# Full-width products of ones on TensorE ahead of norm 1, and one copy that moves on GpSimd

## The chip, the cores and the metric

The kernel runs on one core of one Trainium2 chip. Its time is the device time of one execution in microseconds, and a verdict compares medians of runs. TensorE (PE in the profile) multiplies matrices and writes to PSUM banks; VectorE (DVE), ScalarE (ACT) and GpSimd (POOL) do the elementwise work; SyncE (SP) issues most of the transfers. Each engine works through its own list of instructions in order and waits on semaphores for the others.

## The reference, cut to what matters

One transformer block on 512 tokens of width 1024: an RMS norm, one wide projection that feeds a state-space mixer and a sparse-attention mixer, a gated merge, a convolutional feed-forward part, and a gated embedding. The change touches only the stretch around the first norm and the first projection:

```
def rmsnorm(x, g):
    xf = x.astype(jnp.float32)
    y = xf * lax.rsqrt(jnp.mean(xf * xf, axis=-1, keepdims=True) + EPS)
    return (y * g.astype(jnp.float32)).astype(x.dtype)
...
    n1 = rmsnorm(h, g_mix[i])
    z = n1 @ w_in[i]
```

and, because an instruction of it is moved, the state-space mixer's small tables: `dt = exp(log_dt)`, `a_bar = exp(lam * dt)` and what follows from them.

## The kernel before, in words

The 512 tokens are four tiles of 128 rows (`xts[0..3]`). The gain vector of norm 1 (`grow`, one row of 1024) is spread over 128 partitions by two products of a row of ones with it, into two PSUM banks (`gbs`, L331). Per token tile, the sum of squares goes through `rstd_of` on VectorE (L343, L352, L355), `x_scaled` multiplies the tile by that and by the gains in two halves on VectorE (L300), `t_high` transposes it on TensorE into PSUM (L308) and ScalarE copies it to `n1h`, rounded (L311, by `copy`, L76), and `t_low` takes the remainder `n1l` on VectorE (L316, by `tt`, L55). Three passes of products per tile follow (`v_passes`, L282): `n1h` with the rounded weights, `n1l` with the rounded weights, and, after all tiles, `n1h` with the weights' remainder (`WV` part 1, made by `wv_lo`, L274).

The order on TensorE, VectorE and ScalarE is written by hand in the block from L328 on: an engine's instructions stand there in the order of the code. So on ScalarE the copies of `pps` (the transposed small parameter rows: `prm`, `dcol`) stand ahead of the squares of tile 1, and these ahead of the copies to `n1h` of tile 0. On GpSimd and SyncE, and after this block, a scheduler puts the instructions in order from its own estimates of when each can start.

GpSimd computes the state-space mixer's small vectors (128x16) from `prm`: a chain of two dependent instructions per step of a polynomial (`stg`, `exp_of`, `ts`, `tt`) that starts at `lre` and ends at `rho`, with `kk` and `fl` on the way. VectorE takes them up after the third pass's weights: `ang` from `kk`, `at` from `fl`, then the square of `rho`, and then some thirty small instructions of sine and cosine. Into GpSimd's chain the scheduler puts one instruction that belongs elsewhere: `W2d`, a copy of a 128x64 weight that SyncE loads (`W2`, L711, L714).

`pps` is one of the two PSUM banks with the tag "t" (L336), `ident` a unit matrix, and `sq` a scratch tile for squares.

Of the kernel before, what the change touches and what calls it, by code (L numbers as in the profile page):

```python
# [10 lines left out]
F32R = mybir.dt.float32r  # L11
# [7 lines left out]
P = 128  # L19
# [26 lines left out]
def hybrid_kernel(ctx: ExitStack, tc: tile.TileContext, A, out):  # L46
    nc = tc.nc
    V, G, S, PE = nc.vector, nc.gpsimd, nc.scalar, nc.tensor
# [26 lines left out]
    def copy(o, a):  # L75
        S.activation(o, a, AF.Copy)  # L76
# [10 lines left out]
    def pool(name, bufs=1, side=None, space=None):  # L87
        kw = {"name": name, "bufs": bufs, "reuse_waits": "tile"}
        if side:
            kw["side"] = side  # L90
        if space is not None:
            kw["space"] = space
        return tc.tile_pool(**kw)
# [7 lines left out]
    def bank(tag, name):  # L101
        return psp.tile([P, 512], F32, tag=tag, name=name, bufs=BANKS[tag])
# [17 lines left out]
    def rstd_of(ss, ss2=None, n=1):  # L120

        v, y, t = (small(f"r{c}{n}", n) for c in "vyt")
        ts(v, ss, 0.0 if ss2 is None else ss2, D * EPS, ADD, ADD)
        ts(y.bitcast(I32), v.bitcast(I32), -0.5, FIRST, MUL, ADD)
        for a in NEWTON[:3]:
            if n == 1:
                stt(t, y, v, y, MUL, MUL)
            else:
                tt(t, y, y, MUL)
                tt(t, t, v, MUL)  # L130
            stt(y, t, 3 * a * a, y, SUB, MUL)
        return y
# [6 lines left out]
    def halves(t):  # L139
        return [t[:, i * 512:i * 512 + 512] for i in range(2)]  # L140
# [29 lines left out]
    def last(engine):  # L170
        return next(i for i in reversed(nc.cur_bb.bb.instructions) if i.engine == engine)
# [60 lines left out]
    px = sX.enter_context(pool("x", 1, "right"))  # L232
    xall = slot(cp, "h16", [P, NQ, D], F32, "xall")
    xts = [xall[:, qt] for qt in range(NQ)]
    sq = px.tile([P, D], F32, name="sq")
    wv0 = slot(py, "y8", [P, 2, KD, P], F32, "wv0")
    grow = wv0[0:1, 1].rearrange("p a b -> p (a b)")
    ones = pP.tile([1, P], F32, name="ones")
    G.memset(ones, 1.0)
    grow2 = pP.tile([2 * KD, P], F32, name="grow2")  # L240
    gains = cp.tile([P, 2, KD], F32, name="gains")

# [26 lines left out]
    def wv(x, i):  # L269
        _, w0, w, raw = VCOLS[i]  # L270
        return WV[:, x, :, w0:w0 + w], raw

    def wv_lo(i):
        tt(wv(1, i)[0], wv(1, i)[1], wv(0, i)[0], SUB)  # L274

    def v_passes(qt, passes):
        if qt not in vps:
            vps[qt] = bank(either(), "vps")
        for n in passes:
            nn, x = ((n1h, 0), (n1l, 0), (n1h, 1))[n]  # L280
            for k in range(KD):
                PE.matmul(vps[qt][:, :280], nn[:, k, qt * P:(qt + 1) * P], WV[:, x, k], start=n + k == 0,  # L282
                          stop=n == 2 and k == KD - 1)

    def v_out(qt):
        ps = vps[qt]
        vv = VV[:, qt].rearrange("p b g x d -> p (b g) x d")
        split(vv[:, :, 0], vv[:, :, 1], ps[:, 0:256].rearrange("p (a d) -> p a d", d=HD))
        S.activation(gates[:, qt], ps[:, 256:280], AF.Tanh, scale=0.5)
        ts(gates[:, qt], gates[:, qt], 0.5, 0.5, MUL, ADD)  # L290

    def squared(qt):
        S.activation(sq, xts[qt], AF.Square, accum_out=ss4[:, qt:qt + 1])
# [4 lines left out]
    def x_scaled(qt, r):  # L298
        for i, x in enumerate(halves(xts[qt])):
            stt(x, x, r, gbs[i], MUL, MUL)  # L300

    def t_high(qt):

        res = []
        for b in range(2):
            ps = bank("t", "nt")
            for k in range(4):
                PE.transpose(ps[:, k * P:(k + 1) * P], xts[qt][:, (4 * b + k) * P:(4 * b + k + 1) * P], ident)  # L308
            o = (slice(None), slice(4 * b, 4 * b + 4), slice(qt * P, qt * P + P))
            res.append((o, ps.rearrange("p (k t) -> p k t", k=4)))  # L310
            copy(n1h[o], res[-1][1])  # L311
        return res

    def t_low(res):
        for o, ps in res:
            tt(n1l[o], ps, n1h[o], SUB)  # L316
# [3 lines left out]
    def u_split(ct, part):  # L320
        if not part:
            uw.append([pw.tile([P, KD * P], F32R, name=n, tag=n).rearrange("p (k c) -> p k c", k=KD)
                       for n in ("wh", "wl")])
            copy(uw[ct][0], uraw[ct])
        else:
            tt(uw[ct][1], uraw[ct], uw[ct][0], SUB)

    with tc.manual_schedule(engines={mybir.EngineType.PE, mybir.EngineType.Activation, mybir.EngineType.DVE}):  # L328
        gbs = [bank("s", f"gb{i}") for i in range(2)]
        for ps, g in zip(gbs, halves(grow)):  # L330
            PE.matmul(ps, ones, g, start=True, stop=True)  # L331
        x0 = halves(xts[0])
        S.activation(sq[:, :512], x0[0], AF.Square, accum_out=ss4[:, 0:1])
        V.tensor_tensor_reduce(out=sq[:, 512:], in0=x0[1], in1=x0[1], scale=1.0, scalar=0.0, op0=MUL, op1=ADD,
                               accum_out=ss4[:, NQ:])
        pps = bank("t", "pps")  # L336
        for i in (2, 0, 1):
            PE.transpose(pps[:, i * 16:(i + 1) * 16], prow[:, i], ident[:NPAIR, :NPAIR])
        PE.transpose(pps[:, 48:52], drow, ident[:4, :4])
        copy(*wv(0, 0))  # L340
        copy(prm.rearrange("p a b -> p (a b)"), pps[:, :48])
        copy(dcol, pps[:, 48:52])
        x_scaled(0, rstd_of(ss4[:, 0:1], ss4[:, NQ:]))  # L343
        squared(1)
        t0 = t_high(0)
        V.tensor_copy(*wv(0, 1))
        v_passes(0, (0,))
        t_low(t0)
        v_passes(0, (1,))
        squared(2)  # L350
        squared(3)
        x_scaled(1, rstd_of(ss4[:, 1:2]))  # L352
        t1_ = t_high(1)
        v_passes(1, (0,))
        r = rstd_of(ss4[:, 2:4], n=2)  # L355
        t_low(t1_)
        v_passes(1, (1,))
        x_scaled(2, r[:, 0:1])
        t2_ = t_high(2)
        x_scaled(3, r[:, 1:2])  # L360
        v_passes(2, (0,))
        t3_ = t_high(3)
        t_low(t2_)
        v_passes(2, (1,))
        v_passes(3, (0,))
        t_low(t3_)
        v_passes(3, (1,))
        for i in range(2):
            u_split(i, 0)
        for i in range(2):  # L370
            wv_lo(i)
        u_split(0, 1)
        for qt in range(NQ):
            v_passes(qt, (2,))
            v_out(qt)
            if qt == 1:
                u_split(1, 1)
                trig_at = last(mybir.EngineType.DVE)
# [174 lines left out]
    for lv in range(5):  # L553
        n = 1 << lv
# [32 lines left out]
    for ct in range(4):  # L587
# [3 lines left out]
        for j in range(L):  # L591
            n = L - 1 - j
# [937 lines left out]
```

## Time and profile before

| | |
|---|---|
| median of 3 runs | 828.83 us (828.5 to 829.4) |
| the profiled execution | 829.46 us, of which the span from first to last instruction is 827.5 us |
| TensorE busy | 807.9 us, 98% of the span |
| VectorE, ScalarE, GpSimd busy | 524.3, 393.5, 255.2 us |
| transfers | 83.67 MB, mean 101 GB/s |

The times of rows are microseconds from the start of the span. A row of the timeline gives the start, the length, the engine, the line of the code, the instruction, what it writes and reads, how many it merges, and in brackets the idle time of the engine before it with what ended it. "f32" products with one row of weights take several passes each and appear as two records.

### The profile page before, as it was taken

How to read it: one execution, taken by the hardware profiler on the slowest of the kernel's cores; microseconds unless marked ns; L12 is line 12 of the kernel's file. 1: busy time of each engine (PE TensorE's matmuls, PEld its weight loads, DVE VectorE, ACT ScalarE, POOL GpSimd, SP SyncE). 2: the span in 40 equal slices, each digit the busy share in tenths (PEclk: the TensorE clock that was granted, in tenths of full speed). 3: DMA queues.
4: the chain of work that ended last, by engine and by line, in shares of the span. 5: the costliest groups of instructions: out<-in, count | busy, mean ns of one | idle time of the engine just before them, and what ended most of it. 6: DMA issues, size and time to landing. Idle time of an engine off the chain costs nothing. (4 is left out here: it accounts for less than half of the span.)

```text
span 827.5 us, 12241 instructions
## 1 busy us (share of the span) xinstructions
PE 807.9 (98%) x4529; PEld 677.7 (82%) x4529; DVE 524.3 (63%) x1088; ACT 393.5 (48%) x728; POOL 255.2 (31%) x314
## 2 busy tenths in 40 slices
PE   7999999999999999999999999999999999999996
PEld 5877888878888888888898888888888888888885
DVE  6899988377677640685454444444455947898744
ACT  4437553445777753434354444444434433565522
POOL 6595111124555533131032333333333100000411
PEclk9999999999999999999999999999999999999998
DMA  9663322522333423344052333233323342423011
GB/s 244 161 166 103 91 65 65 129 76 77 77 77 83 148 55 96 109 137 118 2 175 80 103 101 100 86 95 103 99 86 95 121 143 93 153 87 117 26 52 51
DMA packets 112001, 83.67 MB, mean 101 GB/s; under 512 B 9665, under 2 KB 97477, under 8 KB 111942
## 3 DMA queue, kind: packets, MB, share of 16 engines
q1 hardware_dynamic: 111262, 81.82, 34.2%
q10 hardware_dynamic: 680, 1.07, 0.3%
q8 instruction: 36, 0.59, 0.3%
q14 instruction: 23, 0.19, 0.1%
HBM read 75.54 MB, written 3.15 MB: 95 GB/s over the span
## 5 line engine op out<-in xcount | busy, mean ns | idle before, releaser
L55 POOL TENSOR_TENSOR wl<-wr,wh 128x1024 fp32r<-128x1024 f32 x39 | 93.6, 2401 | 246.5 <-ACT wh L76 228.5
L76 ACT ACTIVATE wh<-wr 128x1024 fp32r<-128x1024 f32 x90 | 95.2, 1059 | 95.5 <-issue 32.9
L55 DVE TENSOR_TENSOR wl<-wr,wh 128x1024 fp32r<-128x1024 f32 x51 | 66.0, 1294 | 42.7 <-ACT wh L76 42.7
L83 PE MATMUL pj<-n1h,wh 128*128 128x512 f32 x224 | 92.0, 411 | 0.3 <-ACT un L76 0.3
L85 PE MATMUL pj<-n1h,wl 128*128 128x512 f32 x224 | 88.9, 398 | 0.4 <-DVE wl L55 0.4
L84 PE MATMUL pj<-n1l,wh 128*128 128x512 f32 x224 | 88.6, 396 | 0.0
L64 DVE SCALAR_TENSOR_TENSOR cv<-ub,cvp,cv 128x511 f32<-128x511 f32 (+1 forms) x44 | 32.9, 748 | 66.3 <-ACT cv L1193 65.6
L84 PE MATMUL ua<-n2l,wh 128*128 128x512 f32 (+1 forms) x176 | 67.0, 381 | 0.4 <-DVE n2l L64 0.4
L83 PE MATMUL ua<-n2h,wh 128*128 128x512 f32 (+1 forms) x176 | 67.0, 380 | 0.2 <-ACT n2h L166 0.2
L83 PE MATMUL ub<-n2h,wh 128*128 128x512 f32 (+1 forms) x176 | 66.8, 379 | 0.0
L84 PE MATMUL ub<-n2l,wh 128*128 128x512 f32 (+1 forms) x176 | 66.8, 379 | 0.0
L85 PE MATMUL ub<-n2h,wl 128*128 128x512 f32 (+1 forms) x176 | 66.8, 379 | 0.0
L85 PE MATMUL ua<-n2h,wl 128*128 128x512 f32 (+1 forms) x176 | 66.8, 379 | 0.0
L85 PEld LDWEIGHTS pj<-n1h,wl 128*128 128x128 f32 x224 | 42.4, 189 | 10.3 <-DVE wl L55 1.1
L61 POOL TENSOR_SCALAR pr<-pr,su,gates 128x512 f32<-128x512 f32 (+1 forms) x64 | 38.3, 607 | 37.4 <-DVE su L877 36.3
L84 PEld LDWEIGHTS pj<-n1l,wh 128*128 128x128 f32 x224 | 42.7, 190 | 7.9 <-issue 0.6
L83 PEld LDWEIGHTS pj<-n1h,wh 128*128 128x128 f32 x224 | 42.6, 190 | 7.8 <-ACT un L76 0.6
L874 DVE CUSTOM_DVE_ANT_0 pr<-sps,maskb 128x512 f32<-128x512 f32 (+1 forms) x64 | 30.0, 487 | 18.8 <-PE sps L870 9.4
L55 POOL TENSOR_TENSOR wg1l<-wr,wg1h 128x1024 fp32r<-128x1024 f32 x2 | 7.0, 3514 | 111.5 <-ACT wg1h L76 111.5
L55 DVE TENSOR_TENSOR pl<-ptp,ph 128x128 fp32r<-128x128 f32 (+1 forms) x64 | 31.1, 486 | 14.5 <-ACT ph L76 13.8
L76 ACT ACTIVATE ph<-ptp 128x128 fp32r<-128x128 f32 (+1 forms) x64 | 27.6, 433 | 25.7 <-PE ptp L885 25.0
L84 PEld LDWEIGHTS ua<-n2l,wh 128*128 128x128 f32 x176 | 33.1, 188 | 6.8 <-DVE n2l L64 0.6
(495 smaller groups left out, 2078.0 us busy)
## 6 DMA issues: line engine op xcount, KB each, us to landing
wr<-in_w_up_dram SPq DMA_DIRECT2D x44, 512.0 KB, 3.9
wr<-in_w_in_dram SPq DMA_DIRECT2D x28, 512.0 KB, 4.0
b<-in_w_down_dram SPq DMA_DIRECT2D x12, 512.0 KB, 6.2
wr<-in_w_down_dram SPq DMA_DIRECT2D x10, 512.0 KB, 4.5
QQ<-QT SPq DMA_DIRECT2D x16, 256.0 KB, 3.4
wr<-in_w_out_dram SPq DMA_DIRECT2D x8, 512.0 KB, 4.4
wr<-in_w_ple_gate_dram SPq DMA_DIRECT2D x8, 512.0 KB, 5.3
xall<-in_x_dram SPq DMA_DIRECT2D x4, 512.0 KB
```

Source lines behind the costliest of these rows:

```text
L55: e.tensor_tensor(o, a, b, op=op)
L61: e.tensor_scalar(o, a, s1, s2, op0=op0, op1=op1)
L64: e.scalar_tensor_tensor(o, a, s, b, op0=op0, op1=op1)
L76: S.activation(o, a, AF.Copy)
L83: PE.matmul(ps, lh, rh, start=start, stop=False)
L84: PE.matmul(ps, lh, rl, start=False, stop=False)
L85: PE.matmul(ps, ll, rh, start=False, stop=stop)
L874: V.tensor_tensor_reduce(out=pp, in0=ps[:, :w], in1=maskb[:, T - w:], scale=-(HD ** -0.5), scalar=3e38, op0=ADD, op1=ALU.min, accum_out=nb)
```

## The change

Three things are added and one is moved in the code. VectorE fills a quarter of `sq` with ones and copies it, rounded, to a new tile `sames` (128x256). TensorE multiplies `sames` by itself into the first half of the bank `pps`, 256 columns wide, 16 times ahead of the two products that spread the gains and 4 times behind them. The bank `pps` is taken earlier in the code for that; what stood in it is overwritten by the transposes as before. No result is used.

```
+    sames = px.tile([P, 256], F32R, name="sames")
+    V.memset(sq[:, :256], 1.0)
+    V.tensor_copy(sames, sq[:, :256])
...
         gbs = [bank("s", f"gb{i}") for i in range(2)]
+        pps = bank("t", "pps")
+
+        def busy(n):
+            for _ in range(n):
+                PE.matmul(pps[:, :256], sames[:, :P], sames, start=True, stop=True)
+
+        busy(16)
         for ps, g in zip(gbs, halves(grow)):
             PE.matmul(ps, ones, g, start=True, stop=True)
+        busy(4)
         x0 = halves(xts[0])
...
-        pps = bank("t", "pps")
```

On TensorE, at the start of the program, this is the order before; `gb` are the spread gains, `nt` the transposes of a token tile, `vps` the passes:

```order
L331 MATMUL gb_141<-wv_110,ones 128x512
L331 MATMUL gb_142<-wv_110,ones 128x512
L338 MATMUL pps<-ident,prow 128x16 x3
L339 MATMUL pps<-ident,drow 128x4
L308 MATMUL nt<-ident,xall 128x128 x8
L282 MATMUL vps<-WV,n1h 128x280 x8
```

and this is the order now:

```order
L337 MATMUL pps<-sames 128x256 x16
L341 MATMUL gb_144<-wv_110,ones 128x512
L341 MATMUL gb_145<-wv_110,ones 128x512
L337 MATMUL pps<-sames 128x256 x4
L348 MATMUL pps<-ident,prow 128x16 x3
L349 MATMUL pps<-ident,drow 128x4
L311 MATMUL nt<-ident,xall 128x128 x8
L285 MATMUL vps<-WV,n1h 128x280 x8
```

Twenty products of ones stand around the spread gains; everything else keeps its place.

On GpSimd, in the chain of 128x16 vectors between `lre` and `rho`, the scheduler places the copy of the weight differently, which the code of the change doesn't say:

```order
 L59 TENSOR_SCALAR gtFalse<-kk 128x16
 L55 TENSOR_TENSOR fl<-gtFalse,fl 128x16
+L724 COPY W2d<-W_844 128x128
 L59 TENSOR_SCALAR fl<-fl 128x16
 L59 TENSOR_SCALAR gtFalse<-rd 128x16
...
 L59 TENSOR_SCALAR e1q<-e1r 128x16
 L59 TENSOR_SCALAR gtFalse<-e1q 128x16
-L714 COPY W2d<-W_821 128x128
 L55 TENSOR_TENSOR e1q<-gtFalse,e1r 128x16
```

The copy moves ahead of nine instructions of the chain. On ScalarE and SyncE nothing moves, and on VectorE only the two instructions for `sames` are added, at its very start.

## Rows read from the trace of the kernel before

**Rows 1.** Busy time by engine (PE, PEld, DVE, ACT, POOL), from 27.85 us on.
```profile
27.85:827.50 799.65, 787.05 (x4425) 661.03 (x4425) 505.14 (x1040) 380.50 (x706) 234.75 (x235) 0.99 0.33 97
```

**Rows 2.** Timeline of TensorE, the first 30 us.
```profile
4.82 3.75 PE L331 MATMUL gb<-wv,ones 1*128 1x512 f32 x4 [4.82 <-DMA wv<-in_g_mix_dram]
...
8.82 1.97 PE L308 MATMUL nt<-ident,xall 128*128 128x128 f32 x8
11.66 2.23 PE L282 MATMUL vps<-WV,n1h 128*128 128x280 f32 x8 [0.87 <-ACT n1h L76]
13.69 2.07 PE L282 MATMUL vps<-WV,n1l 128*128 128x280 f32 x8
...
24.74 1.19 PE L282 MATMUL vps<-WV,n1h 128*128 128x280 f32 x8
25.77 1.19 PE L282 MATMUL vps<-WV,n1l 128*128 128x280 f32 x8
27.85 2.33 PE L282 MATMUL vps<-WV,n1h 128*128 128x280 f32 x16 [0.89 <-DVE WV L55]
```

**Rows 3.** Timeline of VectorE, the first 30 us.
```profile
7.28 0.75 DVE L64 SCALAR_TENSOR_TENSOR xall<-xall,ry,gb 128x512 f32<-128x512 f32 x1
...
8.60 0.75 DVE L64 SCALAR_TENSOR_TENSOR xall<-xall,ry,gb 128x512 f32<-128x512 f32 x1 [0.58 <-PE pps L338]
...
11.64 1.29 DVE L55 TENSOR_TENSOR n1l<-nt,n1h 128x512 fp32r<-128x512 f32 x2 [1.56 <-ACT n1h L76]
...
23.99 1.29 DVE L55 TENSOR_TENSOR n1l<-nt,n1h 128x512 fp32r<-128x512 f32 x2 [0.83 <-ACT n1h L76]
...
25.20 2.60 DVE L55 TENSOR_TENSOR WV<-wv,WV 128x1024 fp32r<-128x1024 f32 x2
```

**Rows 4.** Timeline of ScalarE, the first 30 us.
```profile
9.97 1.06 ACT L293 ACTIVATE sq<-xall 128x1024 f32<-128x1024 f32 x1 [0.77 <-DMA xall<-in_x_dram]
...
11.03 1.06 ACT L76 ACTIVATE n1h<-nt 128x512 fp32r<-128x512 f32 x2
```

**Rows 5.** Timeline of GpSimd, its chain from `lre` to `rho`.
```profile
9.23 0.89 POOL L59 TENSOR_SCALAR lre<-prm 128x16 f32<-128x16 f32 x1 [2.98 <-ACT dcol L76]
...
22.29 0.25 POOL L59 TENSOR_SCALAR fl<-fl 128x16 f32<-128x16 f32 x1
...
24.87 0.26 POOL L59 TENSOR_SCALAR gtFalse<-e1q 128x16 f32<-128x16 f32 x1
25.07 0.29 POOL L714 COPY W2d<-W 128x128 f32<-128x128 f32 x1
25.33 1.19 POOL L55 TENSOR_TENSOR e1q<-gtFalse,e1r 128x16 f32<-128x16 f32 x1
...
28.00 1.02 POOL L55 TENSOR_TENSOR e1q<-gtFalse,e1r 128x16 f32<-128x16 f32 x1
29.10 0.25 POOL L59 TENSOR_SCALAR gtFalse<-e1q 128x16 f32<-128x16 f32 x1
...
32.87 0.29 POOL L55 TENSOR_TENSOR rho<-gtFalse,e1s 128x16 f32<-128x16 f32 x1
```

**Rows 6.** Transfers' packets by size, 22.5 to 23, 23 to 23.5, 23.5 to 24 us.
```profile
DMA packets 348, 0.15 MB, mean 304 GB/s; under 512 B 90, under 2 KB 348, under 8 KB 348
...
DMA packets 357, 0.14 MB, mean 277 GB/s; under 512 B 148, under 2 KB 357, under 8 KB 357
...
DMA packets 284, 0.14 MB, mean 280 GB/s; under 512 B 18, under 2 KB 284, under 8 KB 284
```

**Rows 7.** Timelines of VectorE and TensorE, 33 to 57 us.
```profile
33.34 0.16 DVE L55 TENSOR_TENSOR rho<-rho 128x16 f32<-128x16 f32 x1
...
34.16 0.18 DVE L61 TENSOR_SCALAR gates<-gates 128x24 f32<-128x24 f32 x1 [0.28 <-ACT gates L289]
...
40.49 1.23 DVE L55 TENSOR_TENSOR wl<-wr,wh 128x1024 fp32r<-128x1024 f32 x1 [0.81 <-ACT wh L76]
...
56.03 0.50 PE L85 MATMUL pj<-n1h,wl 128*128 128x512 f32 x1 [0.18 <-DVE wl L55]
```

## The prediction, made before the changed kernel had run

> **What bounds the kernel now.** I read the page's busy shares first, then the busy time on both sides of the first long wait, then the timelines of the first 60 us engine by engine. From 27.85 us to the end TensorE is busy 787.05 of 799.65 us [rows 1]: 98%. So the change can move the end only by moving the start of the third passes at 27.85 us, or by opening a new gap on TensorE behind it.
>
> What sets 27.85 is not TensorE. It stands idle there and waits for VectorE's remainder of the weights [rows 2], which VectorE makes in 2.60 us from 25.20 us on [rows 3]. Going back along VectorE, it is idle for 0.83 us ahead of the last `n1l` at 23.99, where it waits on ScalarE's copy, ScalarE on the transposes, and these on VectorE's own scaling two tiles earlier, by then at full pace on TensorE; before that it works without a recorded wait back to the first `n1l` at 11.64 us, ahead of which it waited 1.56 us for ScalarE's `n1h` [rows 3]. ScalarE copies `n1h` at 11.03 us because it was squaring tile 1 from 9.97 on, and that waited 0.77 us for the transfer of tile 1 [rows 4]. The head of the chain is a transfer that the change doesn't touch.
>
> The pace of TensorE in this stretch: eight products of 280 columns start 2.03 us apart from the next eight at 11.66 and 13.69, 254 ns each, and 1.03 us apart at 24.74 and 25.77, 129 ns each [rows 2]. These paces go with the two levels, 1.2 and 2.4 GHz. The products ahead of 11.66 us are the one-row `gb` (3.75 us) and transposes (1.97 us), and after 6 us of these the passes still run at the low level. (The granted clock reads 1.00 in the windows of this stretch too, so the level is read from the pace.)
>
> **The change part by part.**
>
> *The ones.* VectorE's fill and copy stand at its very start, where it waits for the first tile as TensorE waits for the gain vector (4.82 us, [rows 2]). No row shows them; between nothing and a 0.75 us instruction twice as wide [rows 3] each, I take 0.4 each, so that TensorE starts the ones at about 1.6 us. They cost VectorE nothing, since its wait covers them.
>
> *Sixteen products.* 254 ns x 256/280 = 232 ns at the low level: 16 x 0.232 = 3.7 us, from 1.6 to 5.3. The gain vector lands at 4.82, so `gb` starts 0.5 us later than now. If the level has risen by then, `gb` takes 3.75/2 = 1.9 and ends at 7.2, not 8.57; four more products at 129 x 256/280 = 118 ns take 0.5, and the small transposes behind them are done at about 8.1 instead of 8.8, where the large ones begin right behind them [rows 2]. The second half of tile 0 is scaled at 8.03, right behind the first (7.28 + 0.75), not at 8.60: 0.57 us won on VectorE. All of this is won ahead of the wait for tile 1's transfer. ScalarE still starts the squares at 9.97 and the copy of `n1h` at 11.03 [rows 4]; the transposes that this copy needs would have been done at 10.8 anyway (8.82 + 1.97). The two passes at 11.66 and 13.69 would take half their time, but VectorE, not TensorE, sets everything up to 27.85. Gain at the end: 0.
>
> *What comes earlier by it.* GpSimd's chain waits for `dcol`, which ScalarE copies right behind the small transposes; it starts at about 8.5 instead of 9.23 [rows 5].
>
> *The moved copy.* Here I expect a cost. `W2d` now stands where `fl` starts at 22.29, nine steps earlier. With the chain 0.75 us ahead, GpSimd comes to it at 21.5 us. Its weight hasn't landed: `W2` comes in two transfers of 128 rows of 64 numbers, 256 bytes each, the only data packets below 512 B in this stretch, and 90 + 148 + 18 = 256 of them pass from 22.5 to 24.0 us [rows 6]. Its first half alone would be through at 23.2 at the earliest, and before, the copy at 25.07 found it there without a wait [rows 5]. So the bounds are 23.2 and 25.07; I take 24.0, when the last of these packets is through. GpSimd stands still from 21.5 to 24.0, and nine steps of the chain that were behind it by 25.1 are still ahead.
>
> Those then run into a slow stretch. The step of the chain is (24.87 - 22.29)/8 = 0.32 us, but from 25.33 to 29.10 it makes only three, while VectorE makes the weights' remainder from 25.20 on [rows 3, 5]. With the copy done at 24.25, three of the nine fit in before 25.2 and three go through the slow stretch where three others went; six are missing at 29.10, and `rho` comes 6 x 0.325 = 1.95 us later than 33.16 (32.87 + 0.29). VectorE wants it at 33.34 [rows 7] with 0.1 to spare: it stands 1.85 us. Behind `rho` in its order stand the sines, cosines and two remainders of weights. It has 0.28 us of idle time at 34.16 and 0.81 us at 40.49, both for ScalarE [rows 7], to give back: 1.85 - 1.09 = 0.76. After 40.49 VectorE's next recorded wait is behind the remainder that TensorE waits for at 56.03, 0.18 us [rows 7]; so this wait grows by 0.8, and from there on TensorE has no slack that would give it back. With the weight at 23.2 four steps are missing (1.3 - 0.1 - 1.09 = 0.1), with it at 25.07 all nine (2.9 - 0.1 - 1.09 = 1.7).
>
> In the GPSIMD Engine Reference (section Specifications) the Trainium skill says that GpSimd shares its SBUF interfaces with VectorE and is held up by VectorE instructions with two SBUF inputs. The trace agrees: steps take 1.02 to 1.19 us beside `WV<-wv,WV`, and 0.26 us beside `n1l<-nt,n1h`, whose `nt` lies in PSUM [rows 3, 5]. By this rule the cost of the moved copy stands as worked out; were the slow stretch tied to the chain's own steps instead, the wait would have cost nothing, since the chain would walk the 22 steps to `rho` by about 24.25 + 22 x 0.325 = 31.4.
>
> *Sum.* 0 + 0.8 us. Against the profiled execution, 829.46 + 0.8 = 830.3; that execution lay 0.6 above the median of its runs, so I forecast 828.83 + 0.8 = 829.6.
>
> **The rivals.**
>
> *The level doesn't rise in time (+1.1).* The one-row `gb` did not raise it before, so all hangs on the sixteen. Then `gb` ends at 5.3 + 3.75 = 9.05, four more products take 0.9, the small transposes end at 10.5, ScalarE's `prm` and `dcol` behind them at 10.8, and the squares of tile 1, which stand behind these on ScalarE, start 0.8 later than 9.97. The large transposes end at 12.5, the second copy of `n1h` at 13.0 and the second `n1l` at 13.9 instead of 12.9: VectorE's whole chain, and 27.85 with it, 1.0 later. GpSimd reaches the copy when the weight has come, but its chain started 1.6 later: `rho` at 34.8, with VectorE asking at 34.3, inside its slack. 1.0 to 1.2; time 829.9. For it: after 11.66 us of full products it took until at least 13.69 for the pace to change. Against it: the sixteen are products of the very kind that raised it. The Trainium skill (TensorE: Matmul & The Clock Gate, section Part 4: PE-mode transpose) says that transposes don't count as activity as products do; the low passes behind the transposes [rows 2] fit that, and it leaves the ones as the only thing that could count.
>
> *The weight comes late (+1.7, slower).* It decides if `W2` lands at 25 us, as the bound above: VectorE stands 2.8 us at `rho`, TensorE waits 1.9 at 56.03. Time 830.5, about 0.2% above.
>
> *The stall is hidden (0).* If the weight is there by 23.2, or VectorE finds more slack between 40 and 56 us than its recorded waits, the end stays: 828.8.
>
> *TensorE was the bound (faster).* If the low level sets the path, `gb` gives 1.9 and the two passes give (2.03 - 1.03) + (2.07 - 1.19) = 1.9: 825.0. The idle of VectorE ahead of 11.64 and ScalarE's wait for the transfer speak against it.
>
> **How the numbers follow.** Forecast 0.48; level stays low 0.17; late weight 0.14; hidden 0.15; TensorE the bound 0.06. A measurement of this kernel can tell about 0.2%, 1.66 us, from no change. Faster by more than that is the last case alone: 0.06. Slower is most of the late weight and the upper ends of the two cases ahead of it: 0.15. Within it: 0.79. The range runs from 828.4, which takes in the hidden case but for its lower half, to 831.0, above the late weight.
>
> **What would show it.** In the profile of the changed kernel: sixteen products ending near 5.3 us and `gb` in about 2 us; the squares of tile 1 still at 10.0 and the third passes still at 27.8; GpSimd idle ahead of `W2d` for 2 to 3 us until a transfer; VectorE idle ahead of the square of `rho`; and a wait of about 1 us on TensorE near 56 us. The prediction is wrong if the third passes start earlier than 27.3, if `rho` comes before 33.3, or if the wait at 56 us is unchanged.

## The result, and the profile after

The changed kernel takes 835.06 us, the median of 4 runs (832.51 to 835.11), and the kernel before, run beside it, 829.04: the ratio of the means is 1.0066 [1.0046, 1.0086]. It is slower by 6.0 us by the medians, far above the 831.0 at which the predicted range ends; three of the four executions take 835.0 to 835.1, and the fourth, 832.51, lies above the range too. The profiled execution took 835.08 us with a span of 833.1 us.

The busy windows say on which side of the third passes the time was lost. This is the window of the changed kernel from the start of its third passes (columns as in [rows 1]):

```profile
33.52:833.10 799.58, 787.04 (x4425) 660.86 (x4425) 505.00 (x1040) 380.28 (x706) 234.97 (x236) 0.99 0.33 97
```

From there to the end it is 799.58 us, and was 799.65 [rows 1]. The third passes start at 33.52 us, and started at 27.85 [rows 2]: 5.67 later, and this is the whole loss. The timelines of TensorE and ScalarE ahead of them, changed kernel:

```profile
6.23 3.79 PE L337 MATMUL pps<-sames 128*128 128x256 f32 x16 [6.23 <-DVE sames L242]
9.94 3.78 PE L341 MATMUL gb<-wv,ones 1*128 1x512 f32 x4
...
14.80 0.50 PE L348 MATMUL pps<-ident,prow 16*128 16x16 f32 x3
...
17.27 2.02 PE L285 MATMUL vps<-WV,n1h 128*128 128x280 f32 x8
19.13 1.19 PE L285 MATMUL vps<-WV,n1l 128*128 128x280 f32 x8
...
33.52 2.72 PE L285 MATMUL vps<-WV,n1h 128*128 128x280 f32 x19 [0.83 <-DVE WV L55]
...
15.43 0.21 ACT L76 ACTIVATE prm<-pps 128x48 f32<-128x48 f32 x1 [7.55 <-PE pps L349]
...
15.59 1.06 ACT L296 ACTIVATE sq<-xall 128x1024 f32<-128x1024 f32 x1
```

The ones start at 6.23, not at 1.6. The gain vector's products start 5.12 us later than in [rows 2] and still take 3.78: the sixteen products (232 ns apart, the pace of the low level) had not raised the level by their end. Only in the first passes does the pace change, from 2.02 us per eight products to 1.19. ScalarE stands 7.55 us for the small transposes, which are behind all this on TensorE, and squares tile 1 at 15.59, not at 9.97 [rows 4]: 5.62 later. Everything up to the third passes keeps that delay.

Why TensorE starts at 6.23 is on VectorE and GpSimd. Their timelines, changed kernel; `Z` and `CX` are tiles that GpSimd fills with zeros for later:

```profile
0.91 0.27 DVE L241 MEMSET sq<- 128x256 f32 x1 [0.91 <-PEq L1525]
1.22 4.96 DVE L242 CAST sames<-sq 128x256 fp32r<-128x256 f32 x1
...
1.84 0.97 POOL L609 MEMSET Z<- 128x512 f32 x2
...
4.83 1.20 POOL L609 MEMSET CX<- 128x640 f32 x2
5.97 0.34 POOL L298 COPY prow<-dlog 16x128 f32<-16x128 f32 x1
```

The rounding copy of 256 columns took 4.96 us. It ends at 6.18, just behind the last of eight fills that stand without a gap on GpSimd (4.83 + 1.20 = 6.03). The fills are in the kernel before too, but there VectorE's first instruction starts at 4.60, and those beside the last fills were not held: the square of half a tile took 0.69 us, a tensor-scalar instruction of one column 0.21.

The moved copy, which was to cost 0.8 us, cost nothing here. GpSimd and VectorE in the changed kernel:

```profile
15.73 0.27 POOL L59 TENSOR_SCALAR lre<-prm 128x16 f32<-128x16 f32 x1 [9.42 <-ACT dcol L76]
...
28.06 0.29 POOL L724 COPY W2d<-W 128x128 f32<-128x128 f32 x1
...
39.47 0.18 DVE L55 TENSOR_TENSOR rho<-rho 128x16 f32<-128x16 f32 x1 [0.42 <-POOL rho L55]
```

GpSimd's chain starts 6.50 later than in [rows 5], so it comes to the copy long after the weight, and takes it without a wait. VectorE waits 0.42 us for `rho`, inside the slack that it has there: the window above ends no later than before.

### The profile page after: what moved, and what is told of

It reads as the page before. It is cut to its first block, busy times and chain, and to the rows that moved or that the text cites. A ratio compares the mean times of both kernels' runs of the same rounds, so it can differ in the third digit from the quotient of the medians.

```text
span 833.1 us, 12284 instructions
## 1 busy us (share of the span) xinstructions
PE 812.0 (97%) x4549; PEld 680.3 (82%) x4549; DVE 529.4 (64%) x1090; ACT 393.3 (47%) x728; POOL 254.6 (31%) x314
## 3 DMA queue, kind: packets, MB, share of 16 engines
q10 hardware_dynamic: 680, 1.07, 0.3%
```

## The experiments

Behind the third passes kernels can still differ by something that is not the change. In some profiles TensorE's granted clock reads 0.50 for a stretch between 186 and 200 us: in those of the kernel before, of the changed kernel, and of e2, e11, e12 and e13, and not in the eight others. Windows of TensorE (busy time and count, granted clock, DMA share, GB/s), of the kernel before, where the stretch shows, and of experiment e10, where it doesn't:

```profile
188.00:190.00 2.00, 2.00 (x6) 0.50 0.00 0
```
```profile
188.00:190.00 2.00, 1.67 (x10) 1.00 0.00 0
```

Products pass at half the pace there, six in 2.00 us of busy time where e10 has ten in 1.67. From the third passes to the end it is 799.6 us in both kernels with this stretch and 798.7 in e1, e3, e7, e8, e9 and e10, which were profiled without it: it is worth 0.9 us. It comes with the change and without it, and why it comes in some executions only stays open. So profiles are compared by the start of the third passes, and by 798.7 or 799.6 behind it.

The theory on trial: GpSimd's fills hold VectorE's rounding copy, this starts the ones 4.6 us late, and ones and gain products at the low level then stand on the path to tile 1's squares. Rivals: VectorE's own delay does it; the products alone do it wherever they start; the moved copy does it. Edits are against the changed kernel unless it says otherwise. One thing varies along with most of them: the scheduler places `W2d` elsewhere in GpSimd's chain (in e1, e3 and e9 at its old place). Only in e6 does a wait for it reach TensorE; in e7, e10 and e11 VectorE stands 1.07 us for `rho`, and the wait on TensorE that was 0.18 [rows 7] is 0.15 to 0.16.

**e1, the fill and the copy alone.**

```
-        busy(16)
...
-        busy(4)
```

> The changed kernel with VectorE's fill and rounding copy, but without the twenty products. Theory (the rounding copy holds VectorE back, and the late products are what costs): the copy still takes 5 us and tile 0 is squared at 6.1, so the first tile is scaled at 8.8 and 9.6; `gb` starts at 4.8 again, `n1h` of tile 0 comes 0.1 to 0.7 us later than in the kernel before, and the end is 829.2 to 829.8. Rival (the delay of VectorE alone is the cost): 834 to 835 without any product.

829.32 us, ratio 1.0002 [0.9993, 1.0012]. TensorE in e1:

```profile
28.01 4.38 PE L285 MATMUL vps<-WV,n1h 128*128 128x280 f32 x32 [0.85 <-DVE WV L55]
```

The copy still takes 4.96 us and VectorE squares tile 0 at 6.09, but the third passes start at 28.01. A late VectorE alone costs 0.16 us; the path goes through the products.

**e2, the fills twice.** GpSimd writes the same zeros a second time.

```
-    for t in (*ZZ[0], *CX[0], *ZZ[1], *CX[1]):
-        G.memset(t, 0.0)
+    for _ in range(2):
+        for t in (*ZZ[0], *CX[0], *ZZ[1], *CX[1]):
+            G.memset(t, 0.0)
```

> The changed kernel, with GpSimd's eight early fills of Z and CX done twice, some 4.2 us more of GpSimd work at the start. Theory (VectorE's rounding copy waits until GpSimd's fills are over): the copy ends at 10.2 to 10.4 instead of 6.2, the products start there, and the end is about 4.2 us later than the changed kernel, 839. Rival (the copy is slow by itself so early in a program): it ends at 6.2 as before, the end is 835 or, by GpSimd's longer work, at most 836.

837.27 us (835.49 to 838.72), ratio 1.0101 [1.0081, 1.0121]; third passes at 37.01. Its times fall into two pairs, 835.5 and 836.0, 838.6 and 838.7; the profile is one of the upper pair. VectorE, GpSimd and TensorE in it:

```profile
1.22 8.45 DVE L242 CAST sames<-sq 128x256 fp32r<-128x256 f32 x1
...
6.90 2.90 POOL L298 COPY prow<-dlog 16x128 f32<-16x128 f32 x1
...
9.72 3.79 PE L337 MATMUL pps<-sames 128*128 128x256 f32 x16 [9.72 <-DVE sames L242]
```

The scheduler put ten fills ahead of `prow`, up to 6.95, where there were eight, and six behind it. The same copy now takes 8.45 us, and TensorE starts 3.49 later, as the third passes do (37.01 - 33.52). But the copy did not stay held to the last fill, as I had expected: it ended at 9.67, beside the first instruction of GpSimd that isn't a fill. That one, `prow`, itself took 2.90 us instead of 0.34. So the two added fills account for 0.9 us of the 3.49; why copy and `prow` then take 2.8 us beside each other stays open.

**e5, the fills later.** The fills stand behind `rho` on GpSimd.

```
-    for t in (*ZZ[0], *CX[0], *ZZ[1], *CX[1]):
-        G.memset(t, 0.0)
+    with tc.issue_after(rho_at):
+        for t in (*ZZ[0], *CX[0], *ZZ[1], *CX[1]):
+            G.memset(t, 0.0)
```

> The changed kernel, with GpSimd's fills of Z and CX moved behind its `rho`, where it idles 9 us. Theory (the copy waits for the fills): the copy takes 0.2 to 0.4 us, the products run from 1.6 to 5.5; the end is 829 if the clock's level has risen by then, 830 if it has not, and up to 1 us more for fills beside VectorE's tables. Rival (the copy is slow by itself): it takes 5 us again and the end stays near 835.

832.87 us, ratio 1.0053 [1.0038, 1.0068]. VectorE, TensorE and GpSimd in e5:

```profile
1.22 0.85 DVE L242 CAST sames<-sq 128x256 fp32r<-128x256 f32 x1
...
2.12 3.78 PE L337 MATMUL pps<-sames 128*128 128x256 f32 x16 [2.12 <-DVE sames L242]
5.83 3.78 PE L341 MATMUL gb<-wv,ones 1*128 1x512 f32 x4
...
29.42 4.38 PE L285 MATMUL vps<-WV,n1h 128*128 128x280 f32 x32 [0.84 <-DVE WV L55]
...
35.31 0.99 POOL L611 MEMSET Z<- 128x512 f32 x2
...
38.32 1.30 POOL L611 MEMSET CX<- 128x640 f32 x2
...
35.50 0.17 DVE L55 TENSOR_TENSOR den<-lre 128x16 f32<-128x16 f32 x1
35.58 0.17 DVE L529 COPY gains<-ppe 128x16 f32<-128x16 f32 x1
35.67 3.37 DVE L61 TENSOR_SCALAR aq<-ang 128x128 f32<-128x128 f32 x1
...
60.02 0.50 PE L85 MATMUL pj<-n1h,wl 128*128 128x512 f32 x1 [2.61 <-DVE wl L55]
```

Without the eight fills beside it the copy takes 0.85 us, 4.1 less, and the third passes start 4.10 earlier, at 29.42. It ends at 2.07, 0.16 behind the last of the small fills that GpSimd still makes there (1.80 + 0.11 = 1.91); in the changed kernel it ended 0.15 behind the last large one. The end missed the expectation, because the same thing happens again where the fills now stand: VectorE's `aq`, which takes 0.22 us in other kernels, takes 3.37 beside them, and 24 us later TensorE waits 2.61 for a `wl` that stands behind it. That `aq`, which reads and writes SBUF, is held agrees with the Trainium skill (SBUF — State Buffer, section Who interferes with whom): copies, casts and tensor-scalar instructions of VectorE can enter a mode that takes the port pair shared with GpSimd, and the pair goes to whoever issues first, for the whole instruction. Here `aq` stands through more than one instruction of GpSimd: it ends at 39.04, when the eighth fill has just begun. The two-input `den` and the copy of `gains`, which reads PSUM, went through beside the fills. (The square of `rho` behind `aq`, with two inputs, shows 3.23 us from 35.80 on; it ends with `aq`, behind which it stands in VectorE's order.)

**e6, the same rounding with two inputs.** The ones are multiplied by themselves into `sames`, in place of a copy.

```
-    V.tensor_copy(sames, sq[:, :256])
+    tt(sames, sq[:, :256], sq[:, :256], MUL)
```

> The changed kernel, with the rounding done by a product of two inputs (ones times ones) on VectorE in place of the copy. Theory (what waits for GpSimd's fills is this form of instruction, a copy of one input within SBUF; the fills only write, so an instruction with two inputs has nothing to wait for): it takes 0.3 to 0.5 us beside the fills, the products run from 1.7 to 5.5, and the end is 829.0 to 830.5 by the clock's level. Rival (anything that writes SBUF on VectorE through the same path waits for the fills): 5 us again, end 835.

829.84 us (828.98 to 830.62), ratio 1.0015 [1.0005, 1.0024]. VectorE, TensorE and GpSimd in e6:

```profile
1.22 0.58 DVE L55 TENSOR_TENSOR sames<-sq 128x256 fp32r<-128x256 f32 x1
...
1.85 3.78 PE L337 MATMUL pps<-sames 128*128 128x256 f32 x16 [1.85 <-DVE sames L55]
5.57 2.29 PE L341 MATMUL gb<-wv,ones 1*128 1x512 f32 x4
...
27.86 4.38 PE L285 MATMUL vps<-WV,n1h 128*128 128x280 f32 x32 [0.85 <-DVE WV L55]
...
24.82 0.29 POOL L724 COPY W2d<-W 128x128 f32<-128x128 f32 x1 [2.75 <-DMA W<-in_cmp_wk_dram]
...
36.09 0.17 DVE L55 TENSOR_TENSOR rho<-rho 128x16 f32<-128x16 f32 x1 [2.70 <-POOL rho L55]
...
57.45 0.50 PE L85 MATMUL pj<-n1h,wl 128*128 128x512 f32 x1 [1.59 <-DVE wl L55]
```

With GpSimd's fills in their old place, the two-input form takes 0.58 us. The same section of the Trainium skill says that such an instruction contends only with a GpSimd instruction that reads SBUF, and a fill writes; the row agrees. It ends at 1.80, just ahead of the large fills; beside those, `den` of e5 shows that two inputs go through. Here the kernel runs as I had predicted the changed one: ones from 1.85 us, `gb` in 2.29, third passes at 27.86, and the median 1.25 above the kernel before run beside it (828.59), where I had forecast 0.8. The moved copy then costs what was feared of it. GpSimd waits 2.75 us for its weight, VectorE 2.70 us for `rho`, TensorE 1.59 us, where it was 0.18 [rows 7]. From the third passes to the end it is 800.14 us: 1.44 over 798.7.

**e7, without the four products; e8, without the sixteen.**

```
-        busy(4)
```

> The changed kernel without the four products behind `gb`. Theory (from 6.2 us on TensorE's own chain sets ScalarE's squares of tile 1 and the large transposes, at the low level): all behind comes 1.2 us earlier, squares of tile 1 at 14.4, end 833.9, some 5 above the kernel before. Rival (VectorE's wait alone sets the end): unchanged at 835.

```
-        busy(16)
```

> The changed kernel without the sixteen products ahead of `gb`; the slow copy and the four behind stay. Theory: `gb` starts at 4.2 to 4.8 again and ends at 8.6, the four end at 9.8, small transposes at 10.4, squares of tile 1 at 10.5 instead of 10.0, large transposes done at 12.5: end about 1 us above the kernel before, 829.5 to 830. Rival (VectorE's wait alone sets the end): 834 to 835.

e7: 830.75 us, ratio 1.0034 [1.0022, 1.0046]; four executions at 830.6 to 830.8 and two at 832.8 and 833.0. e8: 829.01 us, ratio 1.0005 [0.9996, 1.0014]. TensorE in e7, and in e8:

```profile
6.23 3.59 PE L337 MATMUL pps<-sames 128*128 128x256 f32 x16 [6.23 <-DVE sames L242]
9.74 1.98 PE L341 MATMUL gb<-wv,ones 1*128 1x512 f32 x4
...
29.92 4.25 PE L285 MATMUL vps<-WV,n1h 128*128 128x280 f32 x31 [0.87 <-DVE WV L55]
```
```profile
28.40 0.78 PE L285 MATMUL vps<-WV,n1h 128*128 128x280 f32 x4 [0.88 <-DVE WV L55]
```

e7 missed its 833.9: in its profile the very same sixteen products, from the same 6.23 us, did raise the level (3.59 instead of 3.79, then `gb` in 1.98). So whether they do differs between executions; that its times split by 2 us fits. The four themselves cost 0.83 us there: e13 below, with the level risen too, starts the third passes at 30.75. Without the sixteen, `gb` starts when its vector lands, at 4.88 us, and the four cost 28.40 - 28.01 = 0.39 us over e1, 0.55 over the kernel before; I had expected about 1. The rest of the loss needs the sixteen behind a late copy.

**e3, a fill in bf16.** VectorE fills `sames` directly: no copy, and a tile of its own.

```
-    sames = px.tile([P, 256], F32R, name="sames")
-    V.memset(sq[:, :256], 1.0)
-    V.tensor_copy(sames, sq[:, :256])
+    sames = px.tile([P, 256], mybir.dt.bfloat16, name="sames")
+    V.memset(sames, 1.0)
```

> The changed kernel, with the ones as a bf16 tile made by VectorE's fill alone, no rounding copy; the same twenty products. Theory: the fill takes 0.3 us beside GpSimd's fills, the products run from 1.3 to 5.1, and the end is 829.0 (level high behind them, `gb` in 1.9 us) to 830.2 (level low, `gb` in 3.75, squares of tile 1 at 10.7). Rival (twenty products cost 5 us wherever they start): 834.

828.94 us, ratio 1.0002 [0.9993, 1.0011]. TensorE and ScalarE in e3:

```profile
1.24 3.22 PE L336 MATMUL pps<-sames 128*128 128x256 bf16 x16 [1.24 <-DVE sames L241]
4.61 1.95 PE L340 MATMUL gb<-wv,ones 1*128 1x512 f32 x4
...
8.14 1.97 PE L310 MATMUL nt<-ident,xall 128*128 128x128 f32 x8 [0.70 <-DVE xall L64]
...
27.63 4.41 PE L284 MATMUL vps<-WV,n1h 128*128 128x280 f32 x32 [0.90 <-DVE WV L55]
...
9.76 1.06 ACT L295 ACTIVATE sq<-xall 128x1024 f32<-128x1024 f32 x1 [2.01 <-DMA xall<-in_x_dram]
```

This is the change as it was meant to work: `gb` in 1.95 us, tile 0 scaled by 8.75. And it gains nothing that can be measured, 0.22 us at the third passes, which start at 27.63. ScalarE waits 2.01 us for tile 1 where it waited 0.77 [rows 4], and after a gap of 0.70 us TensorE takes 1.97 us for the transposes, as at the low level in [rows 2]; the level is lost again before the first passes (granted clock 0.84 from 6 to 8 us, 0.50 from 8 to 16).

**e9, ones up to the passes.** e3 with products of ones also behind the small and the large transposes; `beside(n)` is n of them, 232 columns wide, into unused columns of the passes' bank.

```
+        vps[0] = bank(either(), "vps")
...
+        beside(6)
...
+        beside(14)
```

> The bf16 ones by one fill, and beside the twenty products 6 more behind the small transposes and 14 more behind the large ones of tile 0 (232 columns, into unused columns of the passes' bank), so that TensorE is busy until the passes of tile 0. Theory (up to the third passes the end is set by tile 1's transfer and VectorE): passes of tile 0 at the high level, 129 ns each, third passes at 27.4 to 27.9 as in the kernel before, end 828.4 to 829.6. Rival (TensorE's low level is on the path): third passes 2 to 4 us earlier, end 825 to 827.

828.59 us (828.16 to 829.79), ratio 1.0000 [0.9990, 1.0010]. TensorE and VectorE in e9:

```profile
4.92 3.75 PE L346 MATMUL gb<-wv,ones 1*128 1x512 f32 x4
...
14.00 1.27 PE L284 MATMUL vps<-WV,n1h 128*128 128x280 f32 x8
15.11 1.19 PE L284 MATMUL vps<-WV,n1l 128*128 128x280 f32 x8
...
29.05 4.38 PE L284 MATMUL vps<-WV,n1h 128*128 128x280 f32 x32 [0.86 <-DVE WV L55]
...
12.93 1.29 DVE L55 TENSOR_TENSOR n1l<-nt,n1h 128x512 fp32r<-128x512 f32 x2 [2.78 <-ACT n1h L76]
```

The profile is of one of its slower executions (829.67): the level hadn't risen behind the sixteen, and the extra ones stand ahead of the passes. The first two passes start 1.11 us apart, the pace of the high level, but at 14.00 us, and the third passes start at 29.05, 1.20 late, not at 27.4 to 27.9 as expected. From the first `n1l` to the third passes it is 29.05 - 12.93 = 16.12 us, and was 27.85 - 11.64 = 16.21 with the passes 2.03 us apart [rows 2, 3]: what the passes gain in pace moves the third passes by no more than 0.1 us.

**e10, tile 1's transfer first (edit against the kernel before); e11, the same load order on top of e3.** Tile 1 is loaded ahead of the first weights.

```
     xload(0)
...
+    xload(1)
     for c0, w0, w, raw in VCOLS:
...
-    for qt in range(1, NQ):
+    for qt in range(2, NQ):
```

> The kernel before, with the load of tile 1 issued ahead of the loads of the passes' weights. Theory (the head of the chain up to the third passes is tile 1's transfer): ScalarE squares tile 1 at 9.0 to 9.3 instead of 9.97, right behind its small copies, `n1l` of tile 0 starts at 10.9 instead of 11.64, the third passes at 27.2 instead of 27.85, end 0.5 to 0.7 us earlier, 828.0. Rival (something else sets 11.64, the weights' transfers for one): no gain, 828.6 to 829.4, or later by the weights' delay.

> The bf16 ones by one fill, and tile 1 loaded ahead of the weights. Theory: with the transfer out of the way `gb` at the high level lets ScalarE square tile 1 by 9.0 at the latest and the transposes be done by 10.1; third passes at 27.0 to 27.3, end 827.6 to 828.2, 0.1 to 0.4 us better than the same loads without the ones. Rival (the ones never reach the path): the same as without the ones.

e10: 827.87 us (827.61 to 828.59), ratio 0.9990 [0.9981, 0.9999]. e11: 828.64 us, ratio 1.0000 [0.9991, 1.0010]. ScalarE and TensorE in e10:

```profile
9.41 1.06 ACT L294 ACTIVATE sq<-xall 128x1024 f32<-128x1024 f32 x1
...
27.30 4.38 PE L283 MATMUL vps<-WV,n1h 128*128 128x280 f32 x32 [0.85 <-DVE WV L55]
```

In e10 the squares of tile 1 don't wait for the transfer any more; they start 0.56 earlier than in [rows 4] and the third passes 0.55 earlier. It is the fastest version of this study, by 0.8 us of median, of which the profile shows 0.55; an edge so small only just stands clear of its interval. e11 missed at its end: the ones start the third passes 0.33 us earlier still, at 26.97, but its profile has the slow stretch near 187 us (from its third passes to the end of its span of 826.5 it is 799.5), and its median is no better than before.

**e12, e6 with the moved copy behind `rho`; e13, the changed kernel with it there.** The edit of both:

```
-    G.tensor_copy(W2d, W2[:, 0:1].to_broadcast([P, 2, HD]))
+    with tc.issue_after(rho_at):
+        G.tensor_copy(W2d, W2[:, 0:1].to_broadcast([P, 2, HD]))
```

> The ones rounded by an instruction of two inputs, and GpSimd's copy `W2d` pinned behind `rho`. Theory (what the two-input form still lost is the moved copy's wait: 2.75 us on GpSimd, 2.7 on VectorE at `rho`, 1.59 on TensorE near 57 us): VectorE's wait at `rho` and TensorE's wait near 56 us are back at 0 and 0.2, the end 1.2 to 1.4 us earlier, 828.4 to 828.7. Rival (the loss is the products' own): unchanged at 829.8.

> The changed kernel with GpSimd's copy `W2d` pinned behind `rho`. Theory (there the chain starts 6.5 us late and finds the weight landed, so the moved copy costs nothing): 835.0, or 832.5 where the level rises behind the sixteen products, as the changed kernel. Rival (the moved copy is part of the 6 us): 1 to 1.5 us less, 833.6.

e12: 829.23 us (828.28 to 830.79), ratio 1.0005 [0.9995, 1.0015]. e13: 832.29 us (831.64, 832.25, 832.33 and 835.00), ratio 1.0049 [1.0032, 1.0067]. TensorE in e12, and in e13:

```profile
5.57 3.78 PE L341 MATMUL gb<-wv,ones 1*128 1x512 f32 x4
...
57.34 0.50 PE L85 MATMUL pj<-n1h,wl 128*128 128x512 f32 x1 [0.16 <-DVE wl L55]
```
```profile
9.58 1.98 PE L341 MATMUL gb<-wv,ones 1*128 1x512 f32 x4
...
30.75 4.38 PE L285 MATMUL vps<-WV,n1h 128*128 128x280 f32 x32 [0.87 <-DVE WV L55]
```

In e12 the wait near 57 us is back at 0.16. That fits the chain of waits read in e6, from the weight through `rho` to TensorE. But e12 alone doesn't show it: its level stayed low, so its chain on GpSimd starts 2.15 us later than in e6 (11.36, 9.21), and in e5, where it starts as late (11.62) and the copy stands in its new place, GpSimd waits only 0.39 us for the weight. The times of e6 and e12 don't separate, since in e12's profile the level didn't rise behind the ones (`gb` 3.78 from the same 5.57 us, third passes at 29.19, 1.33 later than in e6): that price and the copy's are alike. In e13 the level rose in the profile, and the third passes start 2.77 earlier than in the changed kernel; its one execution at 835.00 is as slow as the changed kernel's three at 835.04 to 835.11. So the copy's place costs the changed kernel nothing. Its single 832.51 lies with e13's three faster ones; that the level rose in it is argued from that, since it has no profile.

## Why the prediction was wrong, by its steps

- **The ones: this step failed.** "I take 0.4 each, so that TensorE starts the ones at about 1.6 us. They cost VectorE nothing, since its wait covers them." The fill took 0.27 us, the copy 4.96. I bounded the copy by the nearest instruction of VectorE, "a 0.75 us instruction twice as wide", and never looked at what GpSimd does in those microseconds: eight fills. e5 (0.85 without them), e6 (0.58 in a form that they don't hold) and, in part, e2 (8.45) show that the fills hold it. VectorE's own chain lost 0.16 us by it (e1), but TensorE started 4.63 us later than I worked with.
- **Sixteen products: the sum was right at each level, the level was not.** 3.7 us was worked out and 3.79 measured. But I had the level risen by their end and gave the other case 0.17, and in the profiled execution it hadn't; e7 and e13 show that it does in some executions and not in others. The rival on the level priced its third passes at 1.0 later, from a start at 1.6. With the copy as it was, 1.0 + 4.63 = 5.6; measured 5.67. e5, with the copy at 0.85, the ones at 2.12 and the level low, starts them 1.57 later: 1.0 + 0.52. So the two causes together make the whole loss, and the copy is the larger: with the level risen behind a late copy (e13) the third passes are still 2.90 late.
- **The gain of a faster `gb`, put at 0: right,** for the reason given. e3 has it and stays within what can be measured, and e10 shows that tile 1's transfer is the head of the chain: take away its wait and 0.55 us comes off. The rival in which TensorE was the bound is refuted: `gb` gives 1.80 us in e3 and the third passes move by 0.22, and the faster passes of e9 move them by no more than 0.1.
- **GpSimd's chain 0.75 us earlier, and the moved copy: not what happened in the changed kernel.** Its chain starts at 15.73, so it comes to `W2d` at 28.06, when the weight has long landed; there was no wait. Where GpSimd does come to the copy ahead of the weight, in e6 (at 22.07, not 21.5; its chain starts at 9.21), the step is right and its size too small: the weight was there at 24.8, not 24.0, VectorE stood 2.70, not 1.85, and the end moved by 1.44, not 0.8. That is nearer to the bound of 1.7. The 24.0 rested on [rows 6], which stop there: from 24.0 to 25.0 the kernel before has 56 more packets below 512 B. The slack of 1.09 us held up: the 1.07 of e10 doesn't reach TensorE, and the 2.70 of e6 reaches it as 1.41.
- **The range** held bounds for the moved copy, but of VectorE's copy only "between nothing and a 0.75 us instruction", and these bounds went into no term of it, because a wait of VectorE was to cover them.

## What to carry to other kernels

Before an instruction is put into an idle stretch of an engine, read what its neighbour does in the same microseconds: here a copy of 0.85 us on VectorE lasted 4.96 beside back-to-back fills on GpSimd, to the end of the fills. Where it must stand there, the two-input form (0.58 us) or a direct fill in the wanted type (0.27 us) did the same work without that wait. And work put ahead of a path to fill idle time becomes the path as soon as it starts late, so its start needs as careful a bound as its length.

## What the runs showed of the hardware that was not expected

- Fills on GpSimd, 0.5 to 0.6 us each, hold one VectorE instruction through a whole row of them: the rounding copy for 4.96 us, to the end of all eight, and `aq` for 3.37, until the eighth begins. Two-input instructions, a copy out of PSUM and, in the kernel before, a tensor-scalar instruction of one column were not held.
- Sixteen full products at one place, from one start, raise TensorE's level in some executions and not in others: `gb` behind them takes 1.98 us in e7 and e13, 3.78 in the changed kernel, 2.29 in e6 and 3.78 in e12; behind sixteen in bf16 1.95 in e3 and 3.75 in e9. What decides stays open.
- In all five profiles in which `gb` ran at the high level (e3, e6, e7, e11, e13) the first passes started at the low one again, and the granted clock reads 0.50 ahead of them or in them. In the others it reads 1.00 through this stretch although the pace is that of the low level, as in the changed kernel up to 17 us: so early in a program the level is to be read from the pace.
- Because the ones were made in `sq`, ScalarE's square of tile 0, which writes `sq`, had to wait for the copy too. Its table load then stands behind a wait: it starts at 4.5 to 4.8 us in the kernels where that is so (4.78 in the changed one; e1, e2, e5 to e8, e12, e13) and at 2.8 in the kernel before and in e3, e9, e10 and e11. ScalarE's square of tile 0 comes 1.6 us later than before, at 6.21 instead of 4.59. Nothing waits for it in the changed kernel, where `gb` is later still; in e5, e6 and e12 VectorE stands 1.40 us for it.
